# Differential attention on one core: a map's scores in one PSUM tile of three joined banks instead of three separate tiles

## The chip, the core and the metric

The kernel runs on one core of a Trainium2 chip. TensorE (PE in the profile, with PEld for its weight loads) multiplies, VectorE (DVE), ScalarE (ACT) and GpSimd (POOL) compute, and SyncE (SP) issues DMAs. Each engine works off its own list of instructions strictly in order; engines wait for each other by semaphores. TensorE writes its results to PSUM, 8 banks of 512 fp32 columns on 128 partitions here. The metric is the device time of one execution in microseconds (us); lower is better.

## The reference

Two layers of a hybrid network over 1024 latent and 256 context tokens: a modulated norm, a projection, three mixers (differential attention, a state-space scan, retention), and an output projection. The change concerns the attention alone:

```python
def diff_attention(q, k, v, lam):
    s = jnp.einsum('bqhmd,bkhmd->bhmqk', q, k).astype(jnp.float32) * (ATT_QK_DIM ** -0.5)
    p = jax.nn.softmax(s, axis=-1)
    a = p[:, :, 0] - lam * p[:, :, 1]
    return jnp.einsum('bhqk,bkhe->bqhe', a.astype(v.dtype), v)
...
    lam_init = 0.8 - 0.6 * math.exp(-0.3 * layer)
    x, ctx = hybrid_layer(x, ctx, c, c_ctx, ...)
```

There are 4 heads. Each head has two maps (`m` = 0, 1), each with its own softmax over 1280 keys; a latent query attends to all 1280 keys, a context query to the 256 context keys alone. The context queries are needed in the first layer only.

## The kernel before

Python code emits instructions for one core, fully unrolled, and a tile scheduler puts them in an order for each engine from its own estimate of their run, with the order in which the code emits them as priority. It adds the semaphores. So the order in the program is fixed at build time.

Most of TensorE's work is the dense projections, emitted by a generator `dense_all` (matmuls at L310 and L312, each product in three matmuls of a split of fp32 into two parts). `phase` (L392) mixes this stream into the mixers: between two `yield`s of a mixer it pumps dense pieces until a budget from the table `SHARE` is spent. Dense results go through two PSUM tiles, `mm`.

The attention is in `head_loop` (L1044): for each of a head's query tiles of 128 rows (8 latent tiles, in layer 0 also 2 context tiles) it calls `head_b` for map 0, `head_c1` and `head_c2` of the tile before, `head_b` for map 1 and `head_c3` of the tile before. That makes 64 latent query tiles with 128 maps of 1280 keys, and 8 context tiles with 16 maps of 256 keys.

`head_b` (L978) computes one map. For each chunk of keys (512, 512, 256) it takes a PSUM tile `s` of one bank from a pool with three buffers, computes the scores with two matmuls (L985), and takes their maximum on VectorE (L987). Then L992 reduces the three maxima to the negative maximum `nb`, and ScalarE does three exponentials (L997), each with the sum of its row in `z`. A buffer comes free for the next map when the exponential of its own chunk is done:

```python
        for ci, (t0, n) in enumerate(chunks):
            nc.scalar.activation(out=em[:, t0:t0 + n], in_=pss[ci][:, 0:n], func=AF.Exp, bias=nb,
                                 accum_out=z[:, 3 * m + ci:3 * m + ci + 1])
```

`head_c1` adds the three sums (`zs`, L1006), takes the reciprocal `rz` (L1010) and the factor `rho` (L1012), and combines the two maps over 1280 columns on VectorE (L1015). `head_c2` transposes the combined map on TensorE (L149, ten transposes into PSUM tiles `t`) and copies the result to `aT` (L116 on ScalarE or L118 on VectorE, in turn). `head_c3` multiplies `aT` with the values (L1036) into the PSUM tile `o`. `head_a` splits and transposes the queries of the tile after next (`qhl`, `qT`).

PSUM holds 2 banks `mm`, 3 `s`, 2 `t` and 1 `o`: all 8. The name `s` is also used outside the attention, by the scans and norms.

Of the kernel before, what the change touches and what calls it, by code (L numbers as in the profile page):

```python
# [9 lines left out]
F32 = mybir.dt.float32  # L10
F32R = mybir.dt.float32r
I32 = mybir.dt.int32
AF = mybir.ActivationFunctionType
ALU = mybir.AluOpType
AX = mybir.AxisListType
PSUM = bass.MemoryType.PSUM
DRAM = bass.MemoryType.DRAM

P = 128
# [3 lines left out]
TOK = 1280  # L23
# [24 lines left out]
def drain(g):  # L48
    for _ in g:
        pass  # L50


class Net:
    def __init__(self, tc, ctx, a, outs):
        self.tc, self.nc, self.a, self.outs = tc, tc.nc, a, outs
        ep = ctx.enter_context
        self.act_p = ep(tc.tile_pool(name="act", bufs=1))
        self.w_p = ep(tc.tile_pool(name="wgt", bufs=2))
        self.u_p = ep(tc.tile_pool(name="unit", bufs=NU))
        self.s_p = ep(tc.tile_pool(name="work", bufs=NW))  # L60
        self.c_p = ep(tc.tile_pool(name="const", bufs=1))
        self.t_p = ep(tc.tile_pool(name="tiny", bufs=2))
        self.d_p = ep(tc.tile_pool(name="dram", bufs=1, space=DRAM))
        self.ps_mm = ep(tc.tile_pool(name="ps_mm", bufs=2, space=PSUM))
        self.ps_s = ep(tc.tile_pool(name="ps_s", bufs=3, space=PSUM))
        self.ps_t = ep(tc.tile_pool(name="ps_t", bufs=2, space=PSUM))
        self.ps_o = ep(tc.tile_pool(name="ps_o", bufs=1, space=PSUM))
        self.uid = 0
        self.flip = 0
        self.queue = []  # L70
        self.ready = []
        self.have = {}
        self.ydone = {}
        self.later = []
        self.pieces = []
        self.wu = []
        self.alive = False
        self.x1k = {}
# [18 lines left out]
    def pmm(self):  # L97
        return self.ps_mm.tile([P, 512], F32, tag="mm", name=self.nm("mm"))

    def pss(self):  # L100
        return self.ps_s.tile([P, 512], F32, tag="s", name=self.nm("s"))

    def pst(self):
        return self.ps_t.tile([P, 512], F32, tag="t", name=self.nm("t"))
# [872 lines left out]

    def head_b(self, qT, kT, m, z, chunks):  # L978
        nc = self.nc
        pss = []  # L980
        mx = self.tiny("mx", 3)
        for ci, (t0, n) in enumerate(chunks):
            ps = self.pss()
            for s in range(2):
                nc.tensor.matmul(ps[:, 0:n], lhsT=qT[:, 2 * m + s, :], rhs=kT[m][:, t0:t0 + n],  # L985
                                 start=(s == 0), stop=(s == 1))
            nc.vector.tensor_reduce(out=mx[:, ci:ci + 1], in_=ps[:, 0:n], axis=AX.X, op=ALU.max,  # L987
                                    negate=len(chunks) == 1)
            pss.append(ps)
        if len(chunks) > 1:  # L990
            nb = self.tiny("nb", 1)
            nc.vector.tensor_reduce(out=nb, in_=mx[:, 0:3], axis=AX.X, op=ALU.max, negate=True)  # L992
        else:
            nb = mx[:, 0:1]
        em = self.unit("e")
        for ci, (t0, n) in enumerate(chunks):
            nc.scalar.activation(out=em[:, t0:t0 + n], in_=pss[ci][:, 0:n], func=AF.Exp, bias=nb,  # L997
                                 accum_out=z[:, 3 * m + ci:3 * m + ci + 1])
        return em

    def head_c1(self, e, z, chunks):
        nc = self.nc
        zv = z.rearrange("p (m c) -> p m c", m=2)
        if len(chunks) > 1:
            zs = self.tiny("zs", 2)
            nc.vector.tensor_reduce(out=zs, in_=zv, axis=AX.X, op=ALU.add)  # L1006
        else:
            zs = zv[:, :, 0]
        rz = self.tiny("rz", 2)
        nc.vector.reciprocal(out=rz, in_=zs)  # L1010
        rho = self.tiny("rho", 1)
        nc.vector.scalar_tensor_tensor(out=rho, in0=zs[:, 0:1], scalar=self.nlam, in1=rz[:, 1:2],  # L1012
                                       op0=ALU.mult, op1=ALU.mult)
        k0 = chunks[0][0]
        nc.vector.scalar_tensor_tensor(out=e[0][:, k0:TOK], in0=e[1][:, k0:TOK], scalar=rho,  # L1015
                                       in1=e[0][:, k0:TOK], op0=ALU.mult, op1=ALU.add)
        return rz

    def head_c2(self, e0, chunks):
        aT = {}  # L1020
        b0 = chunks[0][0] // P

        def sink(j, n, ps):
            t = self.work("aT")
            self.copy(t[:, 0:n * P], ps[:, 0:n * P])
            aT.update({b0 + j + i: t[:, i * P:(i + 1) * P] for i in range(n)})

        self.transposes([e0[:, j * P:(j + 1) * P] for j in range(b0, NT)], sink)
        return aT
# [14 lines left out]
    def head_loop(self, h, last, extra):  # L1044
        post = self.post
        nq = NLT if last else NT
        q, kT = self.heads.pop(h)
        v, = self.need(f"v{h}")
        extra = iter(extra)
        O = self.unit("O", (P, NT, P))  # L1050
        ssq = self.tiny("ossq", NT)
        qTs = {0: self.head_a(q, 0), 1: self.head_a(q, 1)}
        ch = [CHUNKS if i < NLT else CHUNKS[2:] for i in range(nq)]
        st = {}
        for i in range(nq + 1):
            j = i - 1
            if i < nq:
                z = self.t_p.tile([P, 6], F32, tag="z", name=self.nm("z"), bufs=3)
                e0 = self.head_b(qTs[i], kT, 0, z, ch[i])
            if j >= 0:  # L1060
                e, zj = st.pop(j)
                rz = self.head_c1(e, zj, ch[j])
            yield (i + 0.25) / (nq + 1)
            if j >= 0:
                aT = self.head_c2(e[0], ch[j])
            if i + 2 < nq:
                qTs[i + 2] = self.head_a(q, i + 2)
            yield (i + 0.5) / (nq + 1)
            if i < nq:
                e1 = self.head_b(qTs.pop(i), kT, 1, z, ch[i])  # L1070
                st[i] = ((e0, e1), z)
            yield (i + 0.75) / (nq + 1)
            if j >= 0:
                self.head_c3(j, aT, v, rz, O, ssq, ch[j])
            if i < 4:
                next(post, None)
            if i >= nq - AHEAD:
                next(extra, None)
            yield (i + 1) / (nq + 1)
        drain(extra)  # L1080
        drain(post)
        self.post = self.finish_head(O, ssq, f"g{h}", nq, h, 0)
# [301 lines left out]
    def layer(self, l):  # L1384
# [9 lines left out]
        def chain(*gs):  # L1394
            for i, g in enumerate(gs):
                for f in g:
                    yield (i + (f if f is not None else 0.5)) / len(gs)
# [18 lines left out]
            self.phase(self.pair_phase(p, cols, last, extra()), share[p])  # L1416
        self.post = iter(())
        self.phase(chain(prep), share[8])
        for h in range(4):
            ex = self.head_prep(h + 1, last) if h < 3 else ()  # L1420
            self.phase(self.head_loop(h, last, ex), share[9 + h])
        self.phase(self.ret_mix(0, last), share[13])
        self.phase(self.ret_mix(1, last), share[14])
        drain(self.post)
# [53 lines left out]

@with_exitstack
def kernel(ctx: ExitStack, tc: tile.TileContext, a: dict, out: bass.AP):  # L1480
    Net(tc, ctx, a, out).run()


def _layout(inp):
# [80 lines left out]
```

## Time and profile before

| what | value |
|---|---|
| time, median of 3 runs | 2859.37 us (2857.43 to 2861.52) |
| the profiled execution's own time | 2863.47 us |
| its span in the trace | 2861.7 us |
| TensorE busy, share of the span | 94% |
| VectorE, ScalarE, GpSimd busy | 62%, 37%, 27% |
| mean granted TensorE clock | 0.961 |
| attention stages in the span | 631 to 1160 us (layer 0), 2050 to 2556 us (layer 1) |

The span is what the profiler saw of the program; the time is 1.8 us longer. An attention stage is taken from the first score matmul of the layer to the last exponential. The granted clock is a share of full speed: TensorE runs at 2.4 GHz (1.0) or at 1.2 GHz (0.5), and a stretch's figure is a mean over both.

### The profile page before, as it was taken

Reading aid. Unit: us, or ns where it says so; the run is one execution under the profiler, and the core shown is the slowest. Engines: PE = TensorE matmul, PEld = TensorE weight load, DVE = VectorE, ACT = ScalarE, POOL = GpSimd, SP = SyncE. Lnnn points to the kernel's source line nnn. Section 1 sums busy time; section 2 is a strip of 40 time slices with the busy share of each in tenths; the row PEclk is TensorE's granted clock in tenths of the full one; section 3 lists DMA queues with packets and bytes.
Section 4 is the critical chain, followed back from the end, with each engine's and each line's share of the span. In section 5 each row is a group of like instructions: output and inputs, shape, how many; then the busy total and the mean of one; then the engine's idle time right before and its main releaser. Section 6 shows DMA issues by size and latency. Waiting matters only on the chain.

```text
span 2861.7 us, 45083 instructions
## 1 busy us (share of the span) xinstructions
PE 2676.8 (94%) x17116; PEld 2348.5 (82%) x17116; DVE 1771.3 (62%) x4213; ACT 1058.2 (37%) x2678; POOL 777.4 (27%) x688
## 2 busy tenths in 40 slices
PE   7879999999999999998999989998999999999999
PEld 4768877898888898987888767877988888899887
DVE  5567667656677766555445566667567767564651
ACT  3443323224454545332233443323234545442330
POOL 2423233222111121233331423233421122122540
PEclk8979999999999999998999989999999999999999
DMA  6112212222111111033542112121210000102461
GB/s 245 35 35 73 60 48 83 71 64 89 45 54 45 54 31 40 27 103 102 175 159 92 35 39 72 47 60 56 67 32 16 23 16 24 37 18 64 141 210 55
DMA packets 111832, 196.04 MB, mean 69 GB/s; under 512 B 13600, under 2 KB 43104, under 8 KB 111616
## 3 DMA queue, kind: packets, MB, share of 16 engines
q1 hardware_dynamic: 111616, 193.17, 21.4%
q8 instruction: 135, 2.21, 0.3%
q14 instruction: 81, 0.66, 0.1%
HBM read 155.43 MB, written 37.68 MB: 67 GB/s over the span
## 4 chain that ended last, share of the span: by engine, by line
PE 77%; DVE 11%; issue 4%; DMA 3%; ACT 2%; POOL 1%; SPq 0%; DVEq 0%; POOLq 0%; ACTq 0%
PE mm L310 34%; PE mm L312 18%; PE t L149 5%; PE o L1036 4%; PE s L985 4%; PE s L771 2%; PE s L821 2%; DVE mx L987 2%; PE o L814 1%; DMA mr<-mix 1%; PE t L792 1%; ACT e L997 1%; DVE e L1015 1%; DVE cv L512 1%; DVE hu L449 1%
## 5 line engine op out<-in xcount | busy, mean ns | idle before, releaser
L310 PE MATMUL mm<-ah,wh 128*128 128x512 f32 (+1 forms) x1680 | 631.7, 377 | 22.3 <-DVE dtT L546 8.1
L310 PE MATMUL mm<-ah,wl 128*128 128x512 f32 (+1 forms) x1680 | 624.2, 372 | 1.1 <-POOL wl L284 1.1
L310 PE MATMUL mm<-al,wh 128*128 128x512 f32 (+1 forms) x1680 | 624.7, 372 | 0.4 <-DVE al L284 0.4
L284 POOL TENSOR_TENSOR wl<-raw,wh 128x512 fp32r<-128x512 f32 x224 | 295.4, 1338 | 733.4 <-ACT wh L282 717.2
L312 PE MATMUL mm<-wh,ah 128*128 128x256 f32 x1568 | 454.7, 290 | 8.6 <-DVE q L118 7.2
L312 PE MATMUL mm<-wl,ah 128*128 128x256 f32 x1568 | 450.7, 288 | 0.1
L312 PE MATMUL mm<-wh,al 128*128 128x256 f32 x1568 | 449.0, 287 | 0.0
L310 PEld LDWEIGHTS mm<-ah,wh 128*128 128x128 f32 x1680 | 323.7, 193 | 79.6 <-DVE dtT L546 9.5
L310 PEld LDWEIGHTS mm<-ah,wl 128*128 128x128 f32 x1680 | 322.8, 192 | 52.7 <-POOL wl L284 1.6
L310 PEld LDWEIGHTS mm<-al,wh 128*128 128x128 f32 x1680 | 323.4, 193 | 50.0 <-issue 1.2
L312 PEld LDWEIGHTS mm<-wh,ah 128*128 128x128 f32 x1568 | 302.2, 193 | 16.1 <-DVE q L118 7.8
L997 ACT ACTIVATE e<-s,nb 128x512 f32<-128x512 f32 (+1 forms) x384 | 232.1, 614 | 212.6 <-DVE nb L992 210.3
L312 PEld LDWEIGHTS mm<-wl,ah 128*128 128x128 f32 x1568 | 302.4, 193 | 2.7 <-POOL wl L284 0.3
L312 PEld LDWEIGHTS mm<-wh,al 128*128 128x128 f32 x1568 | 302.2, 193 | 2.2
L987 DVE TENSOR_REDUCE mx<-s 128x1 f32<-128x512 f32 (+1 forms) x400 | 224.2, 587 | 53.9 <-PE s L985 52.0
L985 PE MATMUL s<-kT,qT 128*128 128x512 f32 (+1 forms) x800 | 216.7, 376 | 16.0 <-ACT e L997 14.6
L282 ACT ACTIVATE wh<-raw 128x512 fp32r<-128x512 f32 x224 | 130.1, 626 | 215.2 <-DMA raw<-in_wi_dram 98.6
L1036 PE MATMUL o<-v,aT 128*128 128x128 f32 x1312 | 174.1, 276 | 0.2 <-DVE aT L118 0.2
L985 PEld LDWEIGHTS s<-kT,qT 128*128 128x128 f32 x800 | 134.8, 194 | 40.5 <-ACT e L997 26.0
L1036 PEld LDWEIGHTS o<-v,aT 128*128 128x128 f32 x1312 | 163.2, 192 | 4.4 <-DVE v L118 0.8
L765 POOL TENSOR_TENSOR xw<-xn,dtpk 128x512 f32<-128x512 f32 (+2 forms) x96 | 79.7, 842 | 225.6 <-PE s L771 106.8
L793 ACT ACTIVATE t<-t 128x512 f32<-128x512 f32 x144 | 82.2, 583 | 153.4 <-PE t L792 151.4
(281 smaller groups left out, 4539.9 us busy)
## 6 DMA issues: line engine op xcount, KB each, us to landing
raw<-in_wi_dram SPq DMA_DIRECT2D x176, 256.0 KB
wa<-in_wa_dram SPq DMA_DIRECT2D x48, 512.0 KB
E<-cume SPq DMA_DIRECT2D x144, 128.0 KB
mr<-mix SPq DMA_DIRECT2D x64, 256.0 KB
raw<-in_wo_dram SPq DMA_DIRECT2D x32, 256.0 KB
x<-xr SPq DMA_DIRECT2D x26, 256.0 KB
mix<-cv SPq DMA_DIRECT2D x8, 640.0 KB
mix<-sg SPq DMA_DIRECT2D x8, 640.0 KB
```

The source lines that it names most:

```text
L149: self.nc.tensor.transpose(ps[:, j * P:(j + 1) * P], srcs[i + j], self.ident)
L282: nc.scalar.activation(out=hi, in_=x, func=AF.Copy)
L284: e.tensor_tensor(out=lo, in0=x, in1=hi.bitcast(F32), op=ALU.subtract)
L310: nc.tensor.matmul(ps, lhsT=w, rhs=x, start=st, stop=sp)
L312: nc.tensor.matmul(ps, lhsT=x, rhs=w, start=st, stop=sp)
L765: nc.gpsimd.tensor_tensor(out=xw, in0=xn[:, a:a + m].rearrange("p t (h e) -> p t h e", h=2), in1=self.wend[:, a:a + m, h0:h0 + 2].unsqueez ...
L771: nc.tensor.matmul(ps[:, j * P:(j + 1) * P], lhsT=bn[:, c, :], rhs=xw[:, j].rearrange("p h e -> p (h e)"), start=True, stop=True)
L793: nc.scalar.activation(out=ps, in_=ps, func=AF.Exp)
L985: nc.tensor.matmul(ps[:, 0:n], lhsT=qT[:, 2 * m + s, :], rhs=kT[m][:, t0:t0 + n], start=(s == 0), stop=(s == 1))
L987: nc.vector.tensor_reduce(out=mx[:, ci:ci + 1], in_=ps[:, 0:n], axis=AX.X, op=ALU.max, negate=len(chunks) == 1)
L997: nc.scalar.activation(out=em[:, t0:t0 + n], in_=pss[ci][:, 0:n], func=AF.Exp, bias=nb, accum_out=z[:, 3 * m + ci:3 * m + ci + 1])
L1036: nc.tensor.matmul(po[:, 0:P], lhsT=aT[j], rhs=v[:, j, :], start=(j == b0), stop=(j == NT - 1))
```

## The change

During the four heads of a layer the pool `s` is replaced by a pool with a single buffer of 1536 columns, three joined banks (`banks(True)`); after them the pool of three single banks comes back. `head_b` writes the three chunks of a map side by side into this tile, takes a maximum for each chunk as before, and does one exponential over all 1280 columns with one sum. So the sum over chunks in `head_c1` (L1006) falls away. The copies to `aT` no longer alternate: the two of 512 columns go to ScalarE, the last of 256 columns to VectorE.

```diff
+    def banks(self, wide):
+        if self.ps_stack is not None:
+            self.ps_stack.close()
+        self.ps_stack = ExitStack()
+        self.uid += 1
+        self.wide = wide
+        self.ps_s = self.ps_stack.enter_context(
+            self.tc.tile_pool(name=f"ps_s{self.uid}", bufs=1 if wide else 3, space=PSUM))
...
     def pss(self):
-        return self.ps_s.tile([P, 512], F32, tag="s", name=self.nm("s"))
+        return self.ps_s.tile([P, 1536 if self.wide else 512], F32, tag="s", name=self.nm("s"))
...
     def head_b(self, qT, kT, m, z, chunks):
         nc = self.nc
-        pss = []
+        k0 = chunks[0][0]
+        wide = self.pss()
         mx = self.tiny("mx", 3)
         for ci, (t0, n) in enumerate(chunks):
-            ps = self.pss()
+            w = wide[:, t0 - k0:t0 - k0 + n]
             for s in range(2):
-                nc.tensor.matmul(ps[:, 0:n], lhsT=qT[:, 2 * m + s, :], rhs=kT[m][:, t0:t0 + n],
+                nc.tensor.matmul(w, lhsT=qT[:, 2 * m + s, :], rhs=kT[m][:, t0:t0 + n],
                                  start=(s == 0), stop=(s == 1))
-            nc.vector.tensor_reduce(out=mx[:, ci:ci + 1], in_=ps[:, 0:n], axis=AX.X, op=ALU.max,
+            nc.vector.tensor_reduce(out=mx[:, ci:ci + 1], in_=w, axis=AX.X, op=ALU.max,
                                     negate=len(chunks) == 1)
-            pss.append(ps)
...
-        for ci, (t0, n) in enumerate(chunks):
-            nc.scalar.activation(out=em[:, t0:t0 + n], in_=pss[ci][:, 0:n], func=AF.Exp, bias=nb,
-                                 accum_out=z[:, 3 * m + ci:3 * m + ci + 1])
+        nc.scalar.activation(out=em[:, k0:TOK], in_=sc, func=AF.Exp, bias=nb, accum_out=z[:, m:m + 1])
...
-            self.copy(t[:, 0:n * P], ps[:, 0:n * P])
+            self.copy(t[:, 0:n * P], ps[:, 0:n * P], "v" if j == 8 else "a")
...
+        self.banks(True)
         for h in range(4):
             ex = self.head_prep(h + 1, last) if h < 3 else ()
             self.phase(self.head_loop(h, last, ex), share[9 + h])
+        self.banks(False)
```

The order on the engines changes with it, since the scheduler places instructions anew. On TensorE, before, in the last head of layer 1: the six score matmuls of one map (L985), in three PSUM tiles `s`, with dense matmuls between the pairs.

```order
L985 MATMUL s_24973<-kT_23282,qT_24784 128x512 [waits Activation_49]
L985 MATMUL s_24973<-kT_23282,qT_24784 128x512
L312 MATMUL mm_25238<-wh_24675,al_14743 128x256
L312 MATMUL mm_25238<-wh_24675,ah_14742 128x256
L312 MATMUL mm_25238<-wl_24676,ah_14742 128x256
L312 MATMUL mm_25238<-wh_24675,al_14743 128x256
L985 MATMUL s_24977<-kT_23282,qT_24784 128x512 [waits Activation_49]
L985 MATMUL s_24977<-kT_23282,qT_24784 128x512
L312 MATMUL mm_25238<-wh_24675,ah_14742 128x256
L312 MATMUL mm_25238<-wl_24676,ah_14742 128x256
L985 MATMUL s_24981<-kT_23282,qT_24784 128x256 [waits Activation_49]
L985 MATMUL s_24981<-kT_23282,qT_24784 128x256
```

Each pair waits for ScalarE (`Activation_49`), which frees the buffer. TensorE now, in the same head (L997 is the score matmul, L160 the transpose, L1039 the product with the values in the changed file): the end of one query tile, both maps of the next piece by piece.

```order
L997 MATMUL s_24376<-kT_22786,qT_24202 128x512 [waits Activation_49]
L997 MATMUL s_24376<-kT_22786,qT_24202 128x512
L160 MATMUL t_24396<-ident,e_24281 128x128 [waits DVE_49,PE_49]
L160 MATMUL t_24396<-ident,e_24281 128x128 x3
L160 MATMUL t_24403<-ident,e_24281 128x128 [waits PE_49]
L160 MATMUL t_24403<-ident,e_24281 128x128 x3
L997 MATMUL s_24376<-kT_22786,qT_24202 128x512 [waits DVE_49]
L997 MATMUL s_24376<-kT_22786,qT_24202 128x512
```

And a little later on TensorE, the second map of that query tile and the first matmul of the next tile:

```order
L997 MATMUL s_24425<-kT_22961,qT_24202 128x512 [waits Activation_49]
L997 MATMUL s_24425<-kT_22961,qT_24202 128x512
L997 MATMUL s_24425<-kT_22961,qT_24202 128x512 [waits DVE_49]
L997 MATMUL s_24425<-kT_22961,qT_24202 128x512
L997 MATMUL s_24425<-kT_22961,qT_24202 128x256 [waits DVE_49]
L997 MATMUL s_24425<-kT_22961,qT_24202 128x256
L997 MATMUL s_24484<-kT_22786,qT_24310 128x512 [waits Activation_49]
```

The first pair of a map still waits for ScalarE; the second and third pair, which write another bank of the same tile, now wait for VectorE, and no dense matmul stands between. On VectorE now, at the same place (L999 is the maximum, L1005 `nb`, L1013 `rz`, L1018 the combination over 1280 columns):

```order
L999 TENSOR_REDUCE mx_24318<-s_24317 128x1 [waits PE_49] x3
L1005 TENSOR_REDUCE nb_24328<-mx_24318 128x1 [waits DVE_49]
L1013 RECIPROCAL rz_24391<-z_24267 128x2 [waits Activation_49]
L1015 SCALAR_TENSOR_TENSOR rho_24393<-z_24267,nlam_14918,rz_24391 128x1 [waits DVE_49]
L1018 SCALAR_TENSOR_TENSOR e_24281<-e_24330,rho_24393,e_24281 128x1280 [waits DVE_49]
L999 TENSOR_REDUCE mx_24377<-s_24376 128x1 [waits PE_49] x2
L129 COPY aT_24413<-t_24410 128x256 [waits PE_49]
```

The combination of the tile before stands ahead of the next map's first maximum, as it often did before; what is new is that the second score pair waits behind that maximum.

## Rows read from the trace of the kernel before

**Rows 1.** Busy time by stage, the two attention stages: stretch, length, each engine, clock, DMA

```profile
core 0: us, PE busy (x) PEld busy (x) DVE busy (x) ACT busy (x) POOL busy (x), PEclk, DMA share, GB/s
631.00:1160.00 529.00, 504.66 (x3634) 456.10 (x3633) 363.93 (x868) 248.87 (x755) 92.58 (x59) 0.98 0.15 49
2050.00:2556.00 506.00, 480.00 (x3457) 443.77 (x3456) 343.68 (x831) 235.92 (x706) 102.22 (x64) 0.98 0.09 26
```

**Rows 2.** Who waited for whom: total us, times, longest

```profile
PEld s L985 <- ACT e L997: 26.0, 43, 2.4
...
PE s L985 <- ACT e L997: 14.6, 13, 2.2
```

**Rows 3.** Groups by line and shape: total us, mean ns of one, then idle before

```profile
L997 ACT ACTIVATE e<-s,nb 128x512 f32<-128x512 f32 x256 | 173.7, 684 | 212.6 <-DVE nb L992 210.3 <-PE t L149 1.9
...
L997 ACT ACTIVATE e<-s,nb 128x256 f32<-128x256 f32 x128 | 60.7, 474 | 0.0
...
L1006 DVE TENSOR_REDUCE zs<-z 128x2 f32<-128x6 f32 x64 | 10.0, 156 | 61.1 <-ACT e L997 60.6
```

**Rows 4.** Timeline: start us, us; TensorE at 804 and 2378, ScalarE, VectorE

```profile
804.14 0.63 PE L985 MATMUL s<-kT,qT 128*128 128x512 f32 x2
804.61 0.28 PE L312 MATMUL mm<-wh,ah 128*128 128x256 f32 x1
...
2379.39 0.48 PE L985 MATMUL s<-kT,qT 128*128 128x256 f32 x2
2382.09 1.40 PE L985 MATMUL s<-kT,qT 128*128 128x512 f32 x4 [2.22 <-ACT e L997]
...
2381.26 0.69 ACT L997 ACTIVATE e<-s,nb 128x512 f32<-128x512 f32 x1 [1.69 <-DVE nb L992]
2381.85 0.19 ACT L997 ACTIVATION_READ_ACCUMULATOR e<-s,nb 128x1 f32 x1
...
2382.60 0.47 ACT L997 ACTIVATE e<-s,nb 128x256 f32<-128x256 f32 x1
2382.96 0.21 ACT L997 ACTIVATION_READ_ACCUMULATOR e<-s,nb 128x1 f32 x1
...
2385.06 0.41 DVE L987 TENSOR_REDUCE mx<-s 128x1 f32<-128x256 f32 x1
2385.51 0.15 DVE L992 TENSOR_REDUCE nb<-mx 128x1 f32<-128x3 f32 x1
2387.70 0.16 DVE L1006 TENSOR_REDUCE zs<-z 128x2 f32<-128x6 f32 x1 [2.03 <-ACT e L997]
2387.89 0.17 DVE L1010 RECIPROCAL rz<-zs 128x2 f32<-128x2 f32 x1
2388.09 0.22 DVE L1012 SCALAR_TENSOR_TENSOR rho<-zs,nlam,rz 128x1 f32<-128x1 f32 x1
...
2388.62 1.54 DVE L1015 SCALAR_TENSOR_TENSOR e<-e,rho,e 128x1280 f32<-128x1280 f32 x1
```

**Rows 5.** Groups by line and shape, the maxima of 512 columns

```profile
L987 DVE TENSOR_REDUCE mx<-s 128x1 f32<-128x512 f32 x256 | 171.8, 685 | 50.1 <-PE s L985 48.5
```

**Rows 6.** The chain that ended last, 631 to 1160 us: start, us, merged pieces

```profile
660.88 1.14 PE s L985 x6
...
744.41 1.78 PE o L1036 x16
...
762.05 2.87 PE mm L312 x24
...
960.24 1.06 PE t L149 x8
```

**Rows 7.** Busy time in stretches outside the attention with an ill-fed TensorE

```profile
150.00:200.00 50.00, 32.60 (x159) 25.77 (x158) 33.07 (x102) 24.39 (x58) 9.17 (x12) 0.69 0.10 28
1264.00:1335.00 71.00, 57.46 (x274) 49.64 (x273) 54.10 (x97) 22.26 (x50) 33.18 (x33) 0.78 0.50 158
1660.00:1702.00 42.00, 29.51 (x144) 23.73 (x145) 30.30 (x79) 21.34 (x52) 13.85 (x15) 0.67 0.19 55
```

More of the change, by code (lines that the diff above doesn't have):

```diff
@@ L64, in __init__ @@
         self.ps_mm = ep(tc.tile_pool(name="ps_mm", bufs=2, space=PSUM))
-        self.ps_s = ep(tc.tile_pool(name="ps_s", bufs=3, space=PSUM))
         self.ps_t = ep(tc.tile_pool(name="ps_t", bufs=2, space=PSUM))
@@ L69, in __init__ @@
         self.flip = 0
+        self.ps_stack = None
+        self.banks(False)
         self.queue = []
@@ L979, in head_b @@
         nc = self.nc
-        pss = []
+        k0 = chunks[0][0]
+        wide = self.pss()
         mx = self.tiny("mx", 3)
         for ci, (t0, n) in enumerate(chunks):
-            ps = self.pss()
+            w = wide[:, t0 - k0:t0 - k0 + n]
             for s in range(2):
-                nc.tensor.matmul(ps[:, 0:n], lhsT=qT[:, 2 * m + s, :], rhs=kT[m][:, t0:t0 + n],
+                nc.tensor.matmul(w, lhsT=qT[:, 2 * m + s, :], rhs=kT[m][:, t0:t0 + n],
                                  start=(s == 0), stop=(s == 1))
-            nc.vector.tensor_reduce(out=mx[:, ci:ci + 1], in_=ps[:, 0:n], axis=AX.X, op=ALU.max,
+            nc.vector.tensor_reduce(out=mx[:, ci:ci + 1], in_=w, axis=AX.X, op=ALU.max,
                                     negate=len(chunks) == 1)
-            pss.append(ps)
+        sc = wide[:, 0:TOK - k0]
+        nb = mx[:, 0:1]
         if len(chunks) > 1:
@@ L992, in head_b @@
             nc.vector.tensor_reduce(out=nb, in_=mx[:, 0:3], axis=AX.X, op=ALU.max, negate=True)
-        else:
-            nb = mx[:, 0:1]
         em = self.unit("e")
-        for ci, (t0, n) in enumerate(chunks):
-            nc.scalar.activation(out=em[:, t0:t0 + n], in_=pss[ci][:, 0:n], func=AF.Exp, bias=nb,
-                                 accum_out=z[:, 3 * m + ci:3 * m + ci + 1])
+        nc.scalar.activation(out=em[:, k0:TOK], in_=sc, func=AF.Exp, bias=nb, accum_out=z[:, m:m + 1])
         return em
@@ L1002, in head_c1 @@
         nc = self.nc
[L1003 to L1008, printed above, removed]
         rz = self.tiny("rz", 2)
-        nc.vector.reciprocal(out=rz, in_=zs)
+        nc.vector.reciprocal(out=rz, in_=z)
         rho = self.tiny("rho", 1)
-        nc.vector.scalar_tensor_tensor(out=rho, in0=zs[:, 0:1], scalar=self.nlam, in1=rz[:, 1:2],
+        nc.vector.scalar_tensor_tensor(out=rho, in0=z[:, 0:1], scalar=self.nlam, in1=rz[:, 1:2],
                                        op0=ALU.mult, op1=ALU.mult)
@@ L1057, in head_loop @@
             if i < nq:
-                z = self.t_p.tile([P, 6], F32, tag="z", name=self.nm("z"), bufs=3)
+                z = self.t_p.tile([P, 2], F32, tag="z", name=self.nm("z"), bufs=3)
                 e0 = self.head_b(qTs[i], kT, 0, z, ch[i])
@@ L1421, in layer @@
             self.phase(self.head_loop(h, last, ex), share[9 + h])
+        self.banks(False)
         self.phase(self.ret_mix(0, last), share[13])
@@ L1480 @@
 def kernel(ctx: ExitStack, tc: tile.TileContext, a: dict, out: bass.AP):
-    Net(tc, ctx, a, out).run()
+    net = Net(tc, ctx, a, out)
+    net.run()
+    net.ps_stack.close()
 def _layout(inp):
```

## The prediction, made before the changed kernel was run

> **What bounds the kernel now.** The busy times by stage come first: in the two attention stages TensorE is busy 985 of 1035 us at a granted clock of 0.98, VectorE about 68%, ScalarE 47% [rows 1]. TensorE is the bound there, and all its idle time together is 50 us. So the most that shorter work elsewhere can give back is those 50 us; what TensorE loses by new waits is added in full. Next, the list of waits: of the 50 us, score matmuls waiting for an exponential to free a bank take some 26. The weight loads' row has 26.0 us in 43 stops, the matmuls' 14.6 us belong to the same stops [rows 2].
>
> **What the change takes away.** An exponential of 512 columns takes 0.68 us and one of 256 takes 0.47 [rows 3]; with the reading of the sum they end 0.78 and 0.57 us after their start [rows 4]. That is 0.82 ns a column, so one of 1280 columns ends about 0.78 + 768 x 0.82 ns = 1.41 us after its start, where three end after 2382.96 + 0.21 - 2381.26 = 1.91. ScalarE saves 0.5 us for each of 128 maps, 64 us in all; VectorE saves the 64 sums of 0.156 us, 10 us [rows 3]. Neither engine bounds the stage: both savings are worth at most the 26 us of waits. The copies pinned to ScalarE move work of about 0.6 us to an engine that is idle half of the time; I take nothing for them.
>
> **What it adds: two kinds of wait.** One tile instead of three means that the next map's first pair waits for the whole exponential. And in the new order the second and third pair of each map wait for VectorE. All they can wait for there is the maximum of the chunk before in the same tile: before, with a tile each, no such wait stood there. So a map becomes one chain: pair, maximum, pair, maximum, pair, maximum, `nb`, exponential, and only then the next map. Every link in which TensorE has nothing else in its list is idle time.
>
> The price of a link. Two matmuls of 512 columns take 0.63 us until their result is there, and the next matmul starts 0.47 after the first, so the result comes about 0.2 later [rows 4]. The maximum takes 0.69 [rows 5], and two handovers of about 0.05 each (ScalarE to TensorE 2382.04 to 2382.09 [rows 4]) make **1.0 us** from the end of a pair on TensorE to the next pair. From the last pair to the next map: 0.2 for the result, 0.41 and 0.15 for maximum and `nb`, 0.03 to 0.05 at three handovers, 1.41 for the exponential: **2.3 us**. The trace has one place where two maps stand with no work between: TensorE stood 2.22 us, though that wait ended with the first chunk's exponential (0.78, not 1.41) and two other VectorE instructions stood in between [rows 4]. I bound the two prices at 0.8 and 1.9 (results and handovers at nothing) and at 1.2 and 2.7 (one small VectorE instruction in front).
>
> What TensorE has in its list at these places I counted in the new order, with the durations of the chain's merged pieces: 0.12 us for a dense matmul of 256 columns (2.87 / 24), 0.13 for a transpose (1.06 / 8), 0.22 for a product with the values (1.78 / 8, each is two records), 1.14 for six score matmuls [rows 6], and 0.22 for a dense matmul of 512 columns as for a score matmul (0.47 / 2, less a little).
> - Of 256 places between pairs of one map, 75 hold less than 1.0 us of work, 58 of them none. They hold 9 us together: 75 x 1.0 - 9 = **66 us** idle.
> - Of 127 places between a wide map and the next, 86 hold less than 2.3 us, 31 of them none. They hold 53 us: 86 x 2.3 - 53 = **145 us** idle. Before, only 11 of these places held under 1.75 us.
> - In 34 of 64 query tiles the eight transposes of the tile before are all that stands between the first and second pair (the order's second piece). They are counted as cover above, but they need the combination on VectorE, which stands ahead of the first maximum. From the end of the exponential: `rz` and `rho` 0.45 us, the combination 1.54 [rows 4], so 2.0; transposes 1.06 more, so the second pair comes at 3.1. The first pair ends at 0.05 + 0.44, and the transposes fill 1.04: idle 3.1 - 0.49 - 1.04 = 1.57 us, x 34 = **53 us**.
>
> Together 264 us of stops where before there were 26: **+238 us**. With the lower prices and without the third item the sum is 51 + 111 - 26 = +136, with the upper ones and 2.3 us for each of the 34 it is 88 + 179 + 78 - 26 = +319.
>
> **The clock.** In such a tile TensorE has 6.3 us of work (12 score matmuls 2.3, 14 transposes 1.8, ten products 2.2) in about 13.8 us, which the chain laid out by hand gives: 46% busy. Where TensorE was fed badly before, at 65 to 81% busy, the granted clock was 0.69, 0.78 and 0.67 [rows 7]: with two levels, 0.68 means 1.2 GHz for 64% of the time. About 5.3 us of a tile's TensorE work lies on its chain and takes twice as long at 1.2 GHz: 34 x 5.3 x 0.64 = 115 us. The attention stages lose some 20 us already (2% of 1035), about half of it in these tiles: **+105 us**. The bounds are 0 and 34 x 5.3 = 180.
> [...]
>
> A place in the skill speaks against joining the banks: Perfetto Trace Analysis, "Matmuls", wants groups to rotate through different banks so that emptying one overlaps the next group's matmuls. If only that rotation were lost, the first pair would come 1.41 - 0.78 = 0.63 us later at the 86 places, 54 us.
>
> **The sum.** 2863.5 us of the profiled execution + 238 + 105 = 3206; the median of the shown runs lies 4 us lower, so **3202 us**.
>
> **Rivals.**
> - *Stops without a slower clock.* Against it the rows of ill-fed stretches, for it that the covered tiles lie between the bare ones. 2859 + 238 = 3097 us.
> - *The pairs do not wait for the maximum.* If the wait for VectorE is for something long done, the 66 and 53 us are gone and 145 - 26 = 119 remain, with half the clock's loss 2859 + 119 + 50 = 3028. The Trainium skill (PSUM — Partial Sum Buffer, "PSUM bank collisions raise a hardware error") asks for a guard by bank only, and banks 1 and 2 aren't read while the first maximum runs. Against it: the wait stands in the program, wherever a pair of a wide map is second or third.
> - *The stops grow.* VectorE is 68% busy, and copies and norms of the dense stream stand in its list between the maxima. Before, the same counting gives 22 us of stops and the trace has 26, a factor 1.2. With 1.2 x 264 + 2.3 us of combination in place of 1.57 and the clock at 1.2 GHz throughout: 2859 + 317 + 25 - 26 + 180 = 3355 us.
> - *Faster.* The 26 us of waits go, and other idle time of the stages up to 50 us: 2809 to 2833. It needs the chain of a map, at least 2 x 0.44 + 2 x 1.0 + 0.24 + 2.3 = 5.4 us, to lie under other TensorE work in nearly every map; it decides from less than 26 us of uncovered stops on, a tenth of what the order shows.
>
> **How the numbers follow.** The forecast 0.61 (its own range 3140 to 3270), stops without the clock 0.17, growing stops 0.13, free pairs 0.05, faster 0.03, and 0.01 for no change that a measurement can tell (under 0.2%, 6 us). The range 3070 to 3330 holds the forecast, nearly all of the case without the clock and a part of the growing stops: 8 in 10. Slower 0.96, same 0.01, faster 0.03.
>
> **What would show it.** In the waits, score matmuls waiting for the maximum (some 66 us and more, at about 100 places) and for the exponential (145 us, 86 places), where the second kind had 26. In the timeline, an exponential of 1280 columns of 1.3 us plus its sum. In the stages, about 340 us more in the two attention stages, hardly any outside, TensorE busy near three quarters and a granted clock near 0.85 over the stages. I am wrong if the second pairs start while the first maximum still runs, or if the clock stays at 0.98.

## The result, and the profile after

The changed kernel takes 3240.4 us (median of 4 runs, 3233.5 to 3244.1) where the kernel before takes 2860.4 beside it: ratio 1.1328, 95% interval 1.1314 to 1.1342, so 380 us slower. The forecast was 3202 with a range of 3070 to 3330.

The page of the changed kernel first: its span, TensorE's busy tenths in 40 slices, and the granted clock in the same slices.

```profile
span 3241.9 us, 44570 instructions
...
PE   6889999987879887898999899999887877879999
...
PEclk9989999988889898898999899999888978879999
```

The same two rows of the kernel before:

```profile
PE   7879999999999999998999989998999999999999
...
PEclk8979999999999999998999989999999999999999
```

TensorE's row now drops to 7 and 8 in two places, slices 9 to 17 (but for slice 13) and 29 to 36, and the clock drops there in most of the slices. These are the attention stages. Their busy times, with the columns of [rows 1]:

```profile
632.00:1352.00 720.00, 590.78 (x3768) 507.69 (x3768) 363.65 (x825) 233.78 (x529) 91.45 (x62) 0.88 0.11 36
2242.00:2939.00 697.00, 554.53 (x3428) 484.87 (x3427) 331.59 (x765) 216.97 (x464) 94.15 (x65) 0.86 0.06 18
```

Against [rows 1] the stages are 1417 us in place of 1035, so 382 us longer: all of the loss lies here. (The second stretch starts 44 us before the layer's first score matmul in [rows 1] and 30 us before it here. From the first score matmul to the last exponential the two stages are 997 and 1387 us, 390 us longer; TensorE's idle time is 50 and 272 either way.) TensorE's idle time rose from 50 to 272 us, its busy time from 985 to 1145, and the granted clock fell from 0.98 to 0.88 and 0.86. ScalarE is busy 451 us where it was 485. It has less to do, in a longer stage.

Who waited for whom, the matmuls' rows and then the weight loads':

```profile
PE s L997 <- ACT e L1007: 124.4, 79, 3.6
PE t L160 <- DVE e L1018: 61.5, 44, 4.8
PE s L997 <- DVE mx L999: 51.7, 67, 1.7
...
PEld s L997 <- ACT e L1007: 144.6, 84, 3.8
PEld s L997 <- DVE mx L999: 83.3, 75, 2.2
```

In [rows 2] the wait for the exponential had 14.6 us in 13 stops by the first measure and 26.0 in 43 by the second. The wait for the maximum, `mx`, didn't exist. Two groups of the changed kernel, as in [rows 3] and [rows 5]:

```profile
L999 DVE TENSOR_REDUCE mx<-s 128x1 f32<-128x512 f32 x256 | 176.5, 689 | 281.8 <-PE s L997 280.6
L1007 ACT ACTIVATE e<-s,nb 128x1280 f32<-128x1280 f32 x128 | 169.6, 1325 | 336.2 <-DVE nb L1005 336.2
```

The exponential is as cheap as hoped: 1.33 us in place of 2 x 0.68 + 0.47 = 1.84. The maximum costs what it did, 0.69 us. What is new is that VectorE and TensorE wait for each other in turn: VectorE stood 281 us before its maxima, waiting for the scores, where in [rows 5] it stood 50.

One bare tile in the timeline (start us, us, idle before, who ended it), TensorE first, then VectorE, then ScalarE:

```profile
2893.82 0.51 PE L997 MATMUL s<-kT,qT 128*128 128x256 f32 x2 [0.78 <-DVE mx L999]
2896.48 1.22 PE L997 MATMUL s<-kT,qT 128*128 128x512 f32 x2 [2.16 <-ACT e L1007]
2898.61 1.94 PE L160 MATMUL t<-ident,e 128*128 128x128 f32 x8 [0.91 <-DVE e L1018]
2900.21 1.20 PE L997 MATMUL s<-kT,qT 128*128 128x512 f32 x2
...
2907.89 1.21 PE L997 MATMUL s<-kT,qT 128*128 128x512 f32 x2 [2.24 <-ACT e L1007]
2909.88 1.22 PE L997 MATMUL s<-kT,qT 128*128 128x512 f32 x2 [0.78 <-DVE mx L999]
2911.89 0.80 PE L997 MATMUL s<-kT,qT 128*128 128x256 f32 x2 [0.78 <-DVE mx L999]
...
2894.36 0.42 DVE L999 TENSOR_REDUCE mx<-s 128x1 f32<-128x256 f32 x1 [0.60 <-PE s L997]
2894.82 0.16 DVE L1005 TENSOR_REDUCE nb<-mx 128x1 f32<-128x3 f32 x1
2896.46 0.17 DVE L1013 RECIPROCAL rz<-z 128x2 f32<-128x2 f32 x1 [1.49 <-ACT e L1007]
2896.66 0.22 DVE L1015 SCALAR_TENSOR_TENSOR rho<-z,nlam,rz 128x1 f32<-128x1 f32 x1
2896.92 1.55 DVE L1018 SCALAR_TENSOR_TENSOR e<-e,rho,e 128x1280 f32<-128x1280 f32 x1
2898.38 0.68 DVE L999 TENSOR_REDUCE mx<-s 128x1 f32<-128x512 f32 x1
...
2895.01 1.33 ACT L1007 ACTIVATE e<-s,nb 128x1280 f32<-128x1280 f32 x1 [3.99 <-DVE nb L1005]
2896.24 0.19 ACT L1007 ACTIVATION_READ_ACCUMULATOR e<-s,nb 128x1 f32 x1
```

The tile is bare: TensorE has no dense matmul between its pieces. The chain reads from row to row. The last pair of a map ends at 2894.33; its maximum, `nb` and the exponential follow, and the next map's first pair starts at 2896.48, 2.15 us later. Its second pair has to wait behind `rz`, `rho`, the combination and the first maximum, which ends at 2899.06, and then behind eight transposes that take 1.94 us, at a granted clock of 0.50 (shown at the end of this document): it starts 3.7 us after the first. In the following tile the pairs stand 0.78 us apart with nothing between. The maximum takes 0.69 us, and two handovers the rest.

### The profile page after: what moved, and what is told of

The parts are those of the page before. It is cut to its first block, busy times and chain, and to the rows that moved or that the text cites. A ratio compares the mean times of both kernels' runs of the same rounds, so it can differ in the third digit from the quotient of the medians.

```text
span 3241.9 us, 44570 instructions
## 1 busy us (share of the span) xinstructions
PE 2821.5 (87%) x17116; PEld 2423.3 (75%) x17116; DVE 1774.2 (55%) x4113; ACT 1022.7 (32%) x2202; POOL 765.8 (24%) x688
## 4 chain that ended last, share of the span: by engine, by line
PE 71%; DVE 14%; ACT 5%; DMA 4%; issue 4%; POOL 2%; SPq 0%; ACTq 0%; DVEq 0%; POOLq 0%
PE mm L321 29%; PE mm L323 16%; PE t L160 6%; PE s L997 5%; PE o L1039 5%; ACT e L1007 3%; DVE mx L999 3%; DVE e L1018 2%; PE s L832 2%; PE s L782 2%; DMA raw<-in_wi_dram 2%; PE o L825 1%; PE t L803 1%; DMA mr<-mix 1%; POOL wl L295 1%
## 5 line engine op out<-in xcount | busy, mean ns | idle before, releaser
L999 DVE TENSOR_REDUCE mx<-s 128x1 f32<-128x512 f32 (+1 forms) x400 | 237.6, 594 | 455.1 <-PE s L997 453.2
L997 PE MATMUL s<-kT,qT 128*128 128x512 f32 (+1 forms) x800 | 281.2, 437 | 179.0 <-ACT e L1007 124.4
L997 PEld LDWEIGHTS s<-kT,qT 128*128 128x128 f32 x800 | 140.5, 216 | 238.9 <-ACT e L1007 144.6
L1007 ACT ACTIVATE e<-s,nb 128x1280 f32<-128x1280 f32 x128 | 169.6, 1325 | 336.2 <-DVE nb L1005 336.2
L1039 PE MATMUL o<-v,aT 128*128 128x128 f32 x1312 | 196.6, 304 | 1.7 <-ACT aT L127 1.7
L160 PE MATMUL t<-ident,e 128*128 128x128 f32 x656 | 137.0, 358 | 61.6 <-DVE e L1018 61.5
L1039 PEld LDWEIGHTS o<-v,aT 128*128 128x128 f32 x1312 | 187.6, 223 | 3.6 <-ACT aT L127 2.7
L160 PEld LDWEIGHTS t<-ident,e 128*128 128x128 f32 x656 | 107.7, 188 | 97.7 <-issue 54.1
```

The source lines that it names most:

```text
L160: self.nc.tensor.transpose(ps[:, j * P:(j + 1) * P], srcs[i + j], self.ident)
L997: nc.tensor.matmul(w, lhsT=qT[:, 2 * m + s, :], rhs=kT[m][:, t0:t0 + n], start=(s == 0), stop=(s == 1))
L999: nc.vector.tensor_reduce(out=mx[:, ci:ci + 1], in_=w, axis=AX.X, op=ALU.max, negate=len(chunks) == 1)
L1007: nc.scalar.activation(out=em[:, k0:TOK], in_=sc, func=AF.Exp, bias=nb, accum_out=z[:, m:m + 1])
L1039: nc.tensor.matmul(po[:, 0:P], lhsT=aT[j], rhs=v[:, j, :], start=(j == b0), stop=(j == NT - 1))
```

## The experiments

Two theories stood against each other. The **chain theory**: the pairs of a map wait for the maximum of another bank, because the scheduler follows the joined tile as one thing, and these waits bring the stops and the low clock. The **buffer theory**: the score buffer comes free late and all at once, since one exponential has to be done with all three chunks. Diffs are against the kernel named. All kernels compute the whole result, and the kernel before, run beside them, took 2860 to 2862 us.

**The waits between pairs alone**, put into the kernel before: three tiles, three exponentials, copies in turn, and one small copy on VectorE that ties each pair to the maximum of the chunk before.

```diff
             ps = self.pss()
+            if ci:
+                nc.vector.tensor_copy(out=ps[:, 0:1], in_=mx[:, ci - 1:ci])
             for s in range(2):
```

> The kernel before, three tiles and three exponentials, with one thing added: before the second and third pair VectorE writes one column of that pair's tile from the maximum before it, so the pair waits for that maximum. Chain theory: the waits come back without the joined tile; 112 us between pairs, about 70 between maps, about 40 for the combination on VectorE and 70 for the clock: 3060 to 3200 us. Buffer theory: only 256 small VectorE instructions more, 40 us on an engine that is busy 68%: 2860 to 2890 us.

Measured: 3246.2 us, ratio 1.1356 (1.1331 to 1.138), clock 0.915. Its waits and the added copy's group:

```profile
PEld s L987 <- DVE s L985: 91.7, 64, 2.4
PEld s L987 <- ACT e L999: 91.2, 57, 3.3
```

```profile
L985 DVE COPY s<-mx 128x1 f32<-128x1 f32 x256 | 40.7, 159 | 7.6 <-DVE mx L989 0.5
```

This chain of waits gives a loss as large as the change's, with three separate buffers. It is above the range expected, by 46 us. The copies' 0.16 us lie in each link: up to 256 x 0.16 = 41 us, if every one were bare. So the waits without the copies are worth some 345 us or more, an estimate. The chain theory stands; the buffer theory, which had the time near that of before, falls as the main cause.

**The joined tile without these waits.** The changed kernel, with the dependence between a pair and the maxima of other banks declared away; nothing else in the code differs, and the scheduler makes the order anew.

```diff
+        reds = []
...
-                nc.tensor.matmul(w, ...)
+                mm = nc.tensor.matmul(w, ...)
+                for r in reds:
+                    self.tc.declare_no_dep(mm.ins, r.ins, reason="another bank")
...
+            reds.append(red)
```

> The changed kernel with one thing less: the scheduler is told that a pair of score matmuls needs no wait for the maxima of other banks of its tile (they share no column and no bank). One tile, one exponential and pinned copies stay. Chain theory: the order has 15 places under 2.3 us between maps, none of the second and third pairs waits; with a link of about 2.9 us from a map's last pair to the next map the stops are 25 to 30 us, as many as before, and the pinned copies cost 20 us: 2860 to 2900 us. Buffer theory: the first pair's wait for one late release stays, 119 us of stops and more: 2980 us and above.

Measured: 2869.6 us, ratio 1.0037 (1.0019 to 1.0055), clock 0.967. Its stages, its waits for the exponential, and a map in the timeline (TensorE, then VectorE):

```profile
631.00:1165.00 534.00, 502.66 (x3641) 454.89 (x3640) 345.27 (x813) 228.15 (x520) 95.83 (x62) 0.99 0.15 48
2090.00:2560.00 470.00, 438.71 (x3125) 404.91 (x3124) 305.71 (x726) 204.31 (x441) 80.48 (x55) 0.99 0.08 25
```

```profile
PE s L998 <- ACT e L1011: 14.4, 17, 2.3
```

```profile
2121.28 1.30 PE L998 MATMUL s<-kT,qT 128*128 128x512 f32 x6
...
2121.93 0.69 DVE L1002 TENSOR_REDUCE mx<-s 128x1 f32<-128x512 f32 x1 [2.53 <-PE s L998]
...
2123.13 1.02 DVE L1002 TENSOR_REDUCE mx<-s 128x1 f32<-128x512 f32 x2
```

Six score matmuls run through in 1.30 us while VectorE already reads the first bank. That takes 371 of the 380 us away. The joined tile, the single buffer and the one exponential are still there and cost 9 us together.

**Half of the waits.** As above, but only for the second pair; the third still waits (`for r in reds if ci == 1 else ():`).

> The changed kernel with the wait of the second pair taken away as in the run without false waits; the third pair still waits for the maxima of both other banks. Chain theory, by the same counting: 44 places between maps hold less than 2.3 us, 72 us of stops; some 20 us at the third pairs, 20 us for the combination on VectorE, 26 us known from before, 40 us for the clock: 2940 to 3020 us, between the two ends. If one wait in a map is as bad as two, about 3200; if it is free, about 2870.

Measured: 3046.3 us, ratio 1.0654 (1.0637 to 1.0671), clock 0.944.

```profile
PE s L998 <- ACT e L1011: 64.9, 37, 4.9
PE t L160 <- DVE e L1022: 39.4, 31, 4.3
PE s L998 <- DVE mx L1002: 20.7, 21, 3.1
```

Half of the waits bring half of the loss (177 of 371 us), 26 us above the range expected. Each of the three stops of the changed kernel is smaller, also those for the exponential and the combination, which the edit doesn't touch. The order suggests how the stops hang together: work that the scheduler puts between pairs is missing between maps (counted below).

**All six matmuls ahead of the maxima**, in the changed kernel: no maximum stands before a pair of its own map.

```diff
             for s in range(2):
                 nc.tensor.matmul(w, ...)
+        for ci, (t0, n) in enumerate(chunks):
+            w = wide[:, t0 - k0:t0 - k0 + n]
             nc.vector.tensor_reduce(...)
```

> All six score matmuls of a map are emitted ahead of its three maxima, still one joined tile, one exponential, pinned copies. Chain theory (the waits of the second and third pair for the maximum make the loss, directly and by leaving the order without cover): the new order has 14 places under 2.3 us between maps instead of 86; with a link of 3.5 us there (three maxima in a row) the stops are about 40 us, 26 of them known from before: 2860 to 2890 us. Buffer theory (one tile instead of three makes the loss, the first pair waiting for the whole exponential): the stops for the exponential stay near the 124 to 145 us seen, about 3000 us or more.

Measured: 2912.6 us, ratio 1.0183 (1.0168 to 1.0198), clock 0.958.

```profile
PE s L997 <- ACT e L1009: 29.7, 28, 3.4
```

The chain theory's side, but 23 us above its range. Here the first maximum waits for all six matmuls, which lengthens the way to the exponential, and the score matmuls' wait for it is twice that of the kernel without the false waits (14.4 us).

**Late release alone**: the kernel before, with the three exponentials in reverse order, so that the first chunk's buffer comes free last.

```diff
-        for ci, (t0, n) in enumerate(chunks):
+        for ci, (t0, n) in reversed(list(enumerate(chunks))):
```

> The kernel before with the three exponentials of a map in the reverse order, so that the first pair of the next map waits for the last of them, 1.9 us after their start, later than the 1.4 us of one exponential over 1280 columns. Chain theory: the order keeps its cover (18 places under 2.3 us), 0 to 25 us more, 2855 to 2885 us. Buffer theory: late release is the loss, 100 us or more, 2960 us and above.

Measured: 2856.4 us, ratio 0.9993 (0.9979 to 1.0007). With separate buffers the later release costs nothing.

**The pinned copies alone**, in the kernel before.

```diff
-            self.copy(t[:, 0:n * P], ps[:, 0:n * P])
+            self.copy(t[:, 0:n * P], ps[:, 0:n * P], "v" if j == 8 else "a")
```

> The kernel before with the pinned copies of the transposed map alone (two of 512 columns on ScalarE, one of 256 on VectorE). Chain and buffer theory alike: between -10 and +10 us of the kernel before. If the pinned copies have a share in the loss, 20 to 60 us slower.

Measured: 2881.3 us, ratio 1.0072 (1.0057 to 1.0087): 20 us that the prediction put at nothing. **The changed kernel with copies in turn** (the same line, the other way):

> The changed kernel with the copies taking turns again: the joined tile with its waits alone. The pinned copies alone cost 20 us on the kernel before. If that adds up, 3210 to 3225 us; if the copies are hidden in the stops of the chain, 3235 to 3250 us.

Measured: 3247.3 us, ratio 1.136 (1.1341 to 1.1379). In the changed kernel the pinning costs nothing; that the waits hide it is likely and not shown. The same in the **joined tile without the waits, copies in turn**:

> The kernel of the run before this one with the copies of the transposed map taking turns again, as in the kernel before. Chain theory: 10 places under 2.3 us, stops of 20 to 25 us: 2840 to 2870 us, so the joined tile and the one exponential alone are worth nothing or some 10 us. Buffer theory: 2960 us and above.

Measured: 2870.9 us, ratio 1.0037 (1.0023 to 1.005), as with pinned copies. So the 20 us show in the three-buffer kernel alone; no run says why.

**One maximum over all 1280 columns**, copies in turn, in the changed kernel: no maximum can stand between pairs, and `nb` falls away.

```diff
-            nc.vector.tensor_reduce(out=mx[:, ci:ci + 1], in_=w, axis=AX.X, op=ALU.max,
-                                    negate=len(chunks) == 1)
...
-        if len(chunks) > 1:
-            nb = self.tiny("nb", 1)
-            nc.vector.tensor_reduce(out=nb, in_=mx[:, 0:3], axis=AX.X, op=ALU.max, negate=True)
+        nc.vector.tensor_reduce(out=nb, in_=sc, axis=AX.X, op=ALU.max, negate=True)
```

> The changed kernel with a single maximum over all 1280 columns after the six matmuls, without the step that joins three maxima, and with copies taking turns. No pair can wait within a map. The maximum takes about 0.69 + 768 x 1.06 ns = 1.5 us, the link to the next map 0.2 + 1.5 + 1.41 + 0.15 = 3.3 us; 11 places under 2.3 us, 25 us of stops at 3.3: chain theory 2845 to 2880 us, buffer theory 2960 us and above.

Measured: 2864.8 us, ratio 1.0021 (1.0009 to 1.0033). This is the lowest time of the joined versions, and no faster than before.

**Three exponentials again, in the joined tile**, with the waits and without them:

```diff
-        nc.scalar.activation(out=em[:, k0:TOK], in_=sc, func=AF.Exp, bias=nb, accum_out=z[:, m:m + 1])
+        for ci, (t0, n) in enumerate(chunks):
+            nc.scalar.activation(out=em[:, t0:t0 + n], in_=wide[:, t0 - k0:t0 - k0 + n], func=AF.Exp, bias=nb,
+                                 accum_out=z[:, 3 * m + ci:3 * m + ci + 1])
```

> The changed kernel, joined tile and its waits, with three exponentials again and the sum over three. The link between maps grows by 0.5 us; the order has 70 places there that hold less than 2.3 us, so at 2.8 us the stops are about 162 instead of 145 us: chain theory 3250 to 3290 us. If the one exponential is worth nothing, 3230 to 3245.

Measured: 3281.1 us, ratio 1.1473 (1.1452 to 1.1493), 41 us more than with one.

> The run without false waits with three exponentials in place of one: chain theory, ScalarE is off the path there, 2865 to 2890 us against 2870 (17 places under 2.3 us against 15). If the one exponential pays where nothing else waits, 2900 us or more.

Measured: 2931.1 us, ratio 1.0251 (1.0235 to 1.0268), 61 us more than with one. Its stages, and its waits for the exponential and the combination:

```profile
631.00:1200.00 569.00, 522.29 (x3641) 472.17 (x3640) 348.54 (x845) 257.33 (x771) 90.55 (x62) 0.95 0.14 45
2090.00:2630.00 540.00, 494.90 (x3476) 456.79 (x3475) 332.94 (x815) 243.95 (x723) 96.29 (x65) 0.96 0.08 24
```

```profile
PE s L998 <- ACT e L1012: 25.9, 26, 3.5
PE t L160 <- DVE e L1030: 18.9, 13, 2.9
```

The range expected was missed: ScalarE is busy 45% of these stages, yet the three exponentials cost 61 us. TensorE's idle time here is 92 us (569 - 522.3 + 540 - 494.9), where the kernel with one exponential has 63, and the clock falls from 0.99 to 0.95. (The second stretch begins 36 us before the layer's first score matmul, in the kernel with one exponential 7 us, so their idle times can be compared and not their lengths.) So 29 us of the 61 are idle time, and the rest is mostly longer busy time at the lower clock. The stops for the exponential grow by 11.5 us only, from 17 to 26, so most maps don't wait half a microsecond longer: that 61 is near 128 x 0.5 shows nothing. The change's one exponential is worth 41 to 61 us in a single joined buffer, and pays back part of what the joining costs.

## Why the prediction was right

**The place and the mechanism** were as told. All of the time went into the attention stages, 382 us (390 by the other bounds) for 343 forecast. The second and third pairs wait for the maximum. Putting these waits in, with a small copy each, makes the loss; taking them out takes it away, and half of them make half of it. That is shown by three runs, not only argued.

**The stops.** The prediction had 66 us between pairs at 75 places, 145 between maps at 86 and 53 at the combination in 34 tiles: 264. The matmuls' rows have 51.7 in 67 stops, 124.4 in 79 and 61.5 in 44: 238 in 190 stops. In the profile the last matmul before a stop counts as busy until its result is there, 0.63 - 0.47 = 0.16 us [rows 4]; the prediction had this in its prices. With 190 x 0.16 = 30 us the rows give 268. By the same measure the kernel before had 14.6 us and 13 x 0.16, some 17 us, where the prediction took the weight loads' 26. So the term is 251 us and was told as 238. The links themselves were priced well: 0.78 us idle and 0.16 of result time for 1.0, 2.15 and 0.16 from pair to next map for 2.3.

**The clock** was the term most mis-sized, and still near. With two levels, 0.88 of 720 us and 0.86 of 697 us mean 173 and 195 us at 1.2 GHz, where before 0.98 of 1035 us means about 41. TensorE was busy 81% of it now and 95% then, and half of that is lost: 149 - 20 = 129 us, an estimate from these rows, for 105 forecast. Stops and clock together are 251 + 129 = 380, which is the measured difference; that they meet it to the microsecond is luck, since half a hundredth in the clock figures is worth some 6 us. One step of the working had no reason: 0.64, the share of the *time* at 1.2 GHz in other stretches, was used as the share of a tile's *work*. In the five stretches at the end of this document 9.7 of 14.9 us of work, counted at full speed, ran at the low level, 0.66, so the step came out, by luck. The prediction had TensorE busy near three quarters, though its own terms give (985 + 105) / 1378 = 79%, and a clock near 0.85 over the stages; it is 81% and 0.87.

The Trainium skill (TensorE: Matmul & The Clock Gate, "HAM oscillation") tells of a matmul kernel whose batches each start at the low clock, after waits of some 3 to 5 us for a DMA. The stops here are of another kind and shorter, 0.8 to 2.2 us in the timeline above, and the trace has both levels behind a stop: the pair of 256 columns at 2893.82 takes 0.51 us after 0.78 us idle, near the 0.48 of [rows 4], and the pair at 2896.48 takes 1.22 us after 2.16.

**What cost nothing or little.** The shorter exponential and the lost sums were worth nothing against three separate buffers, and the sum gave them nothing: without the false waits the kernel is 9 us slower, not faster. For the pinned copies I took nothing. Alone they cost 20 us, beside the new waits nothing; the sum wasn't harmed, by luck; the step was wrong.

**The rivals.** *Stops without a slower clock* falls with the granted 0.88 and 0.86, *the stops grow* with 268 us where 264 were told, and *faster* with the measured time.
*Pairs that don't wait* falls with the 51.7 us in 67 stops; no second or third pair of a wide map starts before the maximum ahead of it has ended. Its price, 3028 us, kept the 145 us of stops between maps and took away only those between pairs. That fits the order as it stood, and no run has this order without the waits: the kernel without them takes 2870, in an order made anew. From the order on TensorE, with the durations of [rows 6], the kernel before has 619 us of other work between maps and 58 between pairs; the changed kernel has 266 and 462. By the same counting the kernel with half of the waits has some 380 and 325, the one without them some 670 and 1. The scheduler pulled cover into the places between pairs, and put too much in one and none in another: of 256 second and third pairs in the trace 85 start within 0.1 us of the maximum's end, and the median starts 1.1 us after it. Without the waits the cover goes back between the maps.
*Only the rotation lost* was priced at 54 us. The joined tile without the waits loses 9 us. It does lose 71 with three exponentials, so the lost rotation bears on this kernel, and the shorter exponential is what makes up for it. The Trainium skill (Perfetto Trace Analysis, "Matmuls") advises to rotate banks; these two runs, 9 and 71 us slower than before, agree.
The Trainium skill (PSUM — Partial Sum Buffer, "PSUM bank collisions raise a hardware error") asks for a guard by bank. The trace of the kernel without the waits agrees: six score matmuls run into three banks while the first is read, at 2121.93.

**What stays open**: how the 9 us of the joined tile without waits divide between release and order, and why a late release costs nothing in the reversed kernel but 61 us with three exponentials in one tile. In the one the buffers come free one by one, in the other all at once; no run separates that from the order. Of the 61 us only 11.5 are stops for the exponential. Why the pinned copies cost 20 us in the kernel before is open too.

## What to carry to other kernels

A tile that joins several banks is one thing to a scheduler that follows dependences by tile, so writers of one bank can wait for readers of another. Look in the new order for waits that no data asks for, before counting what the larger instruction saves. When such a wait is priced, count the cover that the scheduler moves to it as well: the place that it is taken from is the next stop. An engine far from its limit can still hold the only buffer, and then the length of its work can count.

## What the runs showed that was not expected

The clock changes inside a single bare tile. Busy times of five successive stretches of the changed kernel, with the columns of [rows 1]:

```profile
2880.60:2887.50 6.90, 5.78 (x24) 4.79 (x24) 3.67 (x6) 1.50 (x3) 0.00 (x0) 0.51 0.00 0
2887.50:2894.30 6.80, 3.96 (x24) 2.66 (x23) 2.92 (x6) 1.71 (x4) 0.00 (x0) 1.00 0.00 0
2894.30:2904.50 10.20, 7.13 (x29) 6.12 (x29) 4.14 (x8) 2.61 (x4) 0.00 (x0) 0.50 0.01 2
2904.50:2907.90 3.40, 1.16 (x11) 0.97 (x10) 0.84 (x3) 1.71 (x4) 0.00 (x0) 1.00 0.00 0
2907.90:2918.20 10.30, 6.57 (x20) 4.61 (x20) 4.81 (x10) 1.75 (x4) 0.00 (x0) 0.50 0.04 13
```

In these stretches the granted clock is 0.5 or 1.0 and changes after 3 to 10 us. It falls at 2894.3 and 2907.9, after stretches in which TensorE was busy 58% and 34%, and rises at 2887.5 and 2904.5, after stretches at half speed in which it was busy 84% and 70%. What sets off a change these rows don't show. At the low level two score matmuls take 1.22 us where [rows 4] have 0.63, and eight transposes 1.94 where [rows 6] have 1.06.
